# Summing three adaLN modulation vectors on VectorE instead of TensorE, inside the attention of a two-layer diffusion backbone

## The chip, the cores and the metric

The kernel runs on one core of a Trainium2 chip. The metric is the device time of one execution in microseconds (us); lower is better. A core has TensorE (PE, matrix products), VectorE (DVE), ScalarE (ACT), GpSimd (POOL), SyncE (SP) and 16 DMA engines. Each engine works through its own queue in order, and semaphores make the engines wait for each other.

## The reference

A latent stream of 512 tokens and a context of 256 tokens, 1024 wide, all float32, go through two layers. Layer 0 mixes the tokens by multi-head latent attention with 8 heads, layer 1 by a gMLP with spatial gating; each is followed by a squared-ReLU MLP. Every sub-layer is modulated:

```python
m_lat = (silu_c @ ada_w[i] + ada_b[i])
sh_m, sc_m, g_m, sh_f, sc_f, g_f = jnp.split(m_lat, N_MOD, axis=-1)
h_lat = modulate(x, norm_mix_g[i], sh_m, sc_m)
...
x = x + g_m * o_lat
x = x + g_f * squared_relu_mlp(modulate(x, norm_ffn_g[i], sh_f, sc_f), ffn_w1[i], ffn_w2[i])
```

For each layer there are six modulation vectors of 1024 values (shift, scale and gate, for the mixer and for the MLP). Each is the product of one vector, SiLU(c), with a 1024 x 1024 slice of `ada_w`, 4 MB of weights that are used once.

## The kernel before, in words

Activations lie transposed: channels on the 128 partitions, tokens along the free axis, in eight tiles (KT = 8). Products keep float32 accuracy by splitting both operands into a high and a low part and multiplying three times (`mm3`, lines 79 to 82; `split`, lines 70 to 77: ScalarE casts, VectorE subtracts).

The order of the work is the program's order, rearranged by the framework's scheduler, which lets each engine take the instruction of the lowest priority number that is ready by its own timeline. `with later(BG)` (line 197) raises that number by 400, so that the work in it fills holes. `tc.issue_after(ins)` puts an instruction behind `ins` on its engine.

The first two vectors (shift and scale of layer 0's mixer) are formed at the very start. The other ten are background work, written as a generator, `ada_steps` (lines 154 to 188), in the order of line 155. For each vector:

- eight loads of 128 x 1024 weights (512 KB each), issued by GpSimd (line 161) into a ring of `ada_r` buffers, two during the attention (`AR`, line 37) and three later;
- eight accumulations on VectorE (lines 163 and 165) into one buffer, `acc` (`bufs=1`): each weight tile times the value of SiLU(c) that belongs to its row, so that the vector is the sum of `acc` over the partitions;
- that sum, in one of two ways. The first three vectors (n < BGN = 3: the mixer's gate and the MLP's shift and scale of layer 0) are summed on TensorE: eight matmuls with a block of `acc` as the stationary operand and a column of ones as the moving one (line 182), tied behind the last product of probabilities and values issued so far (`bg_state["pe"]`, set in line 692), and one addition of the bias (line 183). The other seven (`fast`) are transposed in blocks of 32 x 32 into an `ada_r` buffer (line 173), summed along the rows into 32 columns (line 174), brought into place by one matmul with a fixed selection matrix (line 175) and completed by four additions of 32 partitions each (line 178).

The generator yields after each load and accumulation; in the first three vectors there is one more step for the sum, in the other seven the sum is in the step of the last load. So a vector is nine steps or eight, and `left` (line 191) counts 80 + 3.

Each step is called by hand. Ahead of the attention's loop `ada_step(8)` (line 722) asks for the first vector's loads; in the loop over 8 heads x 2 halves of the queries (lines 733 to 741), `ada_step(ADS[i])` (line 737) takes 0, 1 or 2 steps, with `ADS` in line 36, 19 in all. With these 27 steps the three vectors of the attention are done: the first is summed at i = 1, the second at i = 7, the third at i = 13. After it, `tick` (line 204) goes on with the other seven during layer 0's MLP.

In the attention's loop `scores` forms the scores of the next half head on TensorE (line 664) and the softmax on VectorE and ScalarE (lines 668 to 673); `values` transposes the probabilities on TensorE (line 686), splits them and multiplies them with the values. Between them are put pieces of the key and value projection (`kv_proj`), of the query projection (`q_proj`) and of the output projection (`out_proj`, whose `residual`, line 631, is the first user of the first of the three vectors). The powers of -0.5 that the norms need are formed on GpSimd (lines 126, 272, 323), on the same queue as the loads of line 161. A key norm's row goes to DRAM and comes back spread over all partitions (lines 277 and 278).

Of the kernel before, what the change touches and what calls it, by code (L numbers as in the profile page):

```python
# [9 lines left out]
F32 = mybir.dt.float32  # L10
# [3 lines left out]
ALU = mybir.AluOpType  # L14
AX = mybir.AxisListType

P = 128
D = 1024
KT = D // P
# [15 lines left out]
BGN = 3  # L35
ADS = [0, 1, 2, 2, 2, 2, 0, 1, 2, 2, 2, 2, 0, 1, 0, 0]
AR = 2, 3
# [9 lines left out]
def hybrid_dit_kernel(  # L47
# [7 lines left out]
    PE, ACT, DVE, POOL = nc.tensor, nc.scalar, nc.vector, nc.gpsimd  # L55
    SBUF, PSUM = bass.MemoryType.SB, bass.MemoryType.PSUM

    def pool(stack, name, bufs=1, space=SBUF, side="left"):
        return stack.enter_context(tc.tile_pool(name=name, bufs=bufs, space=space, side=side, reuse_waits="tile"))

    @contextmanager
    def later(offset):
        with tc.high_priority(offset=-offset):
            yield

    per = pool(ctx, "per")
# [52 lines left out]
    ones = per.tile([P, P], F32, name="ones")  # L119
# [18 lines left out]
    adab = per.tile([P, 96], F32, name="adab")  # L138
    mod = per.tile([P, 2, 6, KT], F32, name="mod")
# [12 lines left out]
    bg_state = {}  # L152

    def ada_steps():
        order = [(0, 2), (0, 3), (0, 4), (0, 5), (1, 0), (1, 1), (1, 2), (1, 3), (1, 4), (1, 5)]
        for n, (l, ch) in enumerate(order):
            fast = n >= BGN
            acc = bg_state["sb"].tile([P, D], F32, tag="ada_acc", bufs=1, name=f"acc{l}{ch}")
            for k in range(KT):
                r = bg_state["sb"].tile([P, D], F32, tag="ada_r", bufs=AR[fast], name=f"adr{l}{ch}{k}")  # L160
                nc.gpsimd.dma_start(out=r, in_=ada_w[l][k * P:(k + 1) * P, ch * D:(ch + 1) * D])  # L161
                if k == 0:
                    DVE.tensor_scalar(out=acc, in0=r, scalar1=sil[:, 0, 0:1], scalar2=None, op0=ALU.mult)
                else:
                    DVE.scalar_tensor_tensor(out=acc, in0=r, scalar=sil[:, k, 0:1], in1=acc, op0=ALU.mult, op1=ALU.add)  # L165
                if k < KT - 1 or not fast:
                    yield
            i = (l * 6 + ch) * KT
            o = bg_state["pt"](f"adr_o{l}{ch}")
            if fast:  # L170
                r = bg_state["sb"].tile([P, D], F32, tag="ada_r", bufs=AR[fast], name=f"adr{l}{ch}t")
                red = per.tile([P, 32], F32, tag="red", bufs=2, name=f"red{l}{ch}")
                DVE.transpose(out=r, in_=acc)
                DVE.tensor_reduce(out=red, in_=r.rearrange("p (b j) -> p b j", j=32), axis=AX.X, op=ALU.add)
                PE.matmul(o[:, :32], lhsT=sel32, rhs=red, start=True, stop=True)
                for q in range(4):
                    s = slice(32 * q, 32 * q + 32)
                    DVE.tensor_tensor(out=mod[s, l, ch, :], in0=o[s, q:32:4], in1=adab[s, i:i + KT], op=ALU.add)
            else:
                with tc.issue_after(bg_state["pe"]):  # L180
                    for b in range(KT):
                        PE.matmul(o[:, b:b + 1], lhsT=acc[:, b * P:(b + 1) * P], rhs=ones[:, :1], start=True, stop=True)
                DVE.tensor_tensor(out=mod[:, l, ch, :], in0=o[:, :KT], in1=adab[:, i:i + KT], op=ALU.add)
            if ch in (1, 4):
                g = (G_MIX if ch == 1 else G_FFN) + l * KT
                DVE.scalar_tensor_tensor(out=mod[:, l, ch, :], in0=mod[:, l, ch, :], scalar=1.0, in1=cols[:, g:g + KT],
                                         op0=ALU.add, op1=ALU.mult)
            yield

    ada = ada_steps()  # L190
    bg_state.update(left=80 + BGN, keep=80 - 8 * BGN)

    def ada_step(n=1):
        for _ in range(n):
            if bg_state["left"] > bg_state["keep"]:
                bg_state["left"] -= 1
                with later(BG):
                    if "after" in bg_state:
                        with tc.issue_after(bg_state["after"]):
                            next(ada)  # L200
                    else:
                        next(ada)
# [124 lines left out]
    def drain(g, n=100):  # L327
        for _ in range(n):
            if next(g, "end") == "end":
                break  # L330

    nka = KVL + ROPE
    with ExitStack() as ini_stack:
# [7 lines left out]
        def pt(name):  # L341
            return ps.tile([P, 512], F32, tag="t", bufs=2, name=name)

        def pa(name):
            return ps.tile([P, 512], F32, tag="a", bufs=6, name=name)
# [56 lines left out]
        with ExitStack() as xstack:  # L402
# [12 lines left out]
            for k in range(0, KT, 2):  # L415
                o = pa(f"xct{k}")
# [4 lines left out]
            for k in range(KT):  # L421
                o = pa(f"xt{k}")
# [18 lines left out]
        for t in range(NT):  # L441
            o = rp[0][:, t * P:(t + 1) * P] if t < 2 else rp[1][:, (t - 2) * P:(t - 1) * P]
# [5 lines left out]
        def make_h(k):  # L448
            xa = inb.tile([P, TOK], F32, tag="xa", bufs=2, name=f"xa{k}")
            ch = inb.tile([P, CTX], F32R, name="ch", bufs=2)  # L450
            cl = inb.tile([P, CTX], F32R, name="cl", bufs=2)
            for j, src, sl, o_h, o_l in ((1, xcT[:, k, :], slice(0, CTX), ch, cl),
                                         (0, xT[:, k, :], slice(CTX, TOK), hh[k], hl[k])):
                A, B = am[:, k, j:j + 1], bm[:, k, j:j + 1]
                DVE.scalar_tensor_tensor(out=xa[:, sl], in0=src, scalar=A, in1=rsb[:, sl], op0=ALU.mult, op1=ALU.mult)
                ACT.activation(out=o_h, in_=xa[:, sl], func=AF.Identity, bias=B)
                DVE.scalar_tensor_tensor(out=o_l, in0=xa[:, sl], scalar=B, in1=o_h.bitcast(F32),
                                         op0=ALU.add, op1=ALU.subtract)
            return ch, cl

        kva = None
        for k in range(KT):
# [6 lines left out]
            ch, cl = make_h(k)  # L469
            for t in range(NT):  # L470
                a_h, a_l = (ch, cl) if t < 2 else (hh[k], hl[k])
                s = bass.ts(t if t < 2 else t - 2, P)
# [5 lines left out]
        for k in range(0, KT, 2):  # L478
            r = W.load(wq_a, k, 2, 0, QL, f"wqa{k}")
# [27 lines left out]
        for u in range(3):  # L507
            st = ini.tile([P, 4, 2], F32, name="kst", bufs=3)
            us = slice(2 * u, 2 * u + 2)
            for j in range(2):  # L510
                t = 2 * u + j
# [4 lines left out]
            o = pt(f"ckt{u}").rearrange("p (k n) -> p k n", k=2)  # L516
            for j in range(2):
                t = 2 * u + j
# [4 lines left out]
            s = slice(2 * u * P, (2 * u + 2) * P)  # L523
# [26 lines left out]
        for t in range(NL):  # L550
            o = qas[t] if t in qas else query_latent(t)
# [83 lines left out]
    with hst as st_:  # L635
# [83 lines left out]
                    residual(0, 2, 2 * dq + d, o, s_)  # L719
                    n0.add(2 * dq + d, half)  # L720

        drain(q_proj(0)); ada_step(8)
        steps = [(h, half) for h in range(HEADS) for half in range(2)]
        scores(0, 0)
        fill = {}
# [133 lines left out]
    with ExitStack() as st_:  # L859
# [7 lines left out]
        for q in range(4):  # L867
            ws = [W(gm_w_in, 2 * k2, 2, HALF + q * 512, 512, f"gv{q}{k2}") for k2 in range(4)]
            for ts in ((0, 1), (2, 3)) if q == 0 else ((0, 1, 2, 3),):
                acc = {t: (pu if t < 2 else pd)(f"v{q}{t}") for t in ts}  # L870
                for k in range(KT):
                    wh, wl = ws[k // 2]
                    for t in ts:
                        s = slice(t * P, (t + 1) * P)
                        mm3(acc[t], hs[k][0][:, s], hs[k][1][:, s], wh[:, k % 2, :], wl[:, k % 2, :], k == 0, k == KT - 1)
                for t in ts:
# [8 lines left out]
                            in_=gm_bs.rearrange("g p -> (g p)").unsqueeze(0).to_broadcast([P, G * P]))  # L885
        for g4 in range(2):
            o = pt(f"wst{g4}")
# [6 lines left out]
            o = pt(f"rsw{g4}")  # L894
# [121 lines left out]
```

## Time and profile before

| | us |
|---|---|
| median of 3 runs | 1373.73 |
| lowest, highest | 1372.16, 1377.34 |
| the profiled execution | 1371.87 |
| its span, first to last instruction | 1370.1 |
| PE busy in the span | 1330.4 (97%) |
| PEld (weight loads) busy | 1138.0 (83%) |
| DVE busy | 850.4 (62%) |
| ACT busy | 536.5 (39%) |
| POOL busy | 88.6 (6%) |

The busy times are of that one execution. PE is TensorE's matmuls and PEld its weight loads, which overlap with matmuls. Matmuls are pipelined and their ends are modelled, so a PE that is busy all the time is not a PE at its peak. The chain of waits follows the work that ended last back from the end: at each step to what released it, or to the instruction before it on its engine. "issue" is time for which the profile shows no cause. "<-" after an idle time names the engine and the tile that ended it.

### The profile page before, as it was taken

The numbers are of one execution on the slowest core, as the hardware profiler recorded it, in microseconds if no ns is written. First come the engines' busy times: TensorE is split into PE (matmuls) and PEld (weight loads), VectorE is DVE, ScalarE is ACT, GpSimd is POOL, SyncE is SP. The second block draws the span as 40 slices with busy tenths as digits, with TensorE's granted clock in tenths as the row PEclk, the third lists the DMA queues.
The fourth block names the chain that finished last, engine by engine and source line by source line (L and its number), as shares of the span: only waits on it lengthen the run. The fifth ranks groups of instructions, "written<-read, shape, count | busy, mean of one in ns | idle before, by whom it ended". The sixth has DMA issues, their size and how long they took to land.

```text
span 1370.1 us, 18200 instructions
## 1 busy us (share of the span) xinstructions
PE 1330.4 (97%) x7055; PEld 1138.0 (83%) x7055; DVE 850.4 (62%) x1409; ACT 536.5 (39%) x1022; POOL 88.6 (6%) x137
## 2 busy tenths in 40 slices
PE   6988899999899999999999999999999999999998
PEld 4888899999888888888897888888888888888888
DVE  5886988888998887434574456445574344343452
ACT  7565566555631322313343333222353132231331
POOL 2031200200111110000000010000000000000000
PEclk9999999999999999999999999999999999999999
DMA  8741411412688876232232232232223233333211
GB/s 267 229 149 61 135 61 53 141 64 74 191 279 267 278 248 214 93 93 92 92 109 92 77 123 77 77 93 92 62 77 111 92 99 98 103 96 94 92 46 62
DMA packets 128070, 166.38 MB, mean 121 GB/s; under 512 B 7643, under 2 KB 111712, under 8 KB 127984
## 3 DMA queue, kind: packets, MB, share of 16 engines
q1 hardware_dynamic: 116032, 122.67, 28.2%
q0 software_dynamic: 11808, 42.03, 9.7%
q8 instruction: 55, 0.90, 0.3%
q10 hardware_dynamic: 144, 0.52, 0.1%
q14 instruction: 31, 0.25, 0.1%
HBM read 163.08 MB, written 2.12 MB: 121 GB/s over the span
## 4 chain that ended last, share of the span: by engine, by line
PE 85%; DVE 4%; issue 4%; DMA 3%; ACT 3%; POOL 0%; SPq 0%; DVEq 0%; ACTq 0%; POOLq 0%
PE s L664 3%; PE v L82 2%; PE v L80 2%; PE v L81 2%; DMA adr<-in_ada_w_dram 1%; PE f1d2o L80 1%; PE f1d0o L81 1%; PE f1d0o L80 1%; PE f1d0o L82 1%; PE f1d2o L81 1%; PE f1d2o L82 1%; PE f0d0o L80 1%; PE f0d1o L81 1%; PE f0d1o L80 1%; PE f0d1o L82 1%
## 5 line engine op out<-in xcount | busy, mean ns | idle before, releaser
L165 DVE SCALAR_TENSOR_TENSOR acc<-adr,sil,acc 128x1024 f32<-128x1024 f32 x70 | 89.6, 1280 | 20.2 <-DMA adr<-in_ada_w_dram 19.8
L161 POOL DMA_DIRECT2D adr<-in_ada_w_dram x80 | 43.0, 538 | 269.3 <-DVE acc L165 121.3
L812 DVE TENSOR_TENSOR f1a<-f1a 128x512 f32<-128x512 f32 (+1 forms) x36 | 22.5, 629 | 39.8 <-ACT f1a L811 39.8
L72 ACT CAST f0uh<-f0a 128x512 fp32r<-128x512 f32 (+1 forms) x36 | 20.4, 572 | 51.4 <-DVE f0a L812 51.4
L668 DVE CUSTOM_DVE_ANT_0 p<-s,rk,rq 128x768 f32<-128x768 f32 x32 | 32.4, 1013 | 8.0 <-DMA rk<-rkd 4.2
L73 DVE TENSOR_TENSOR tl<-pt,th 128x512 fp32r<-128x512 f32 x48 | 31.9, 684 | 6.1 <-ACT th L72 5.8
L671 ACT ACTIVATE p<-p,sm 128x768 f32<-128x768 f32 x32 | 30.1, 941 | 13.3 <-DVE sm L670 13.3
L126 POOL TENSOR_TENSOR nst<-nst,mhalf 128x2 f32<-128x2 f32 x6 | 5.1, 855 | 454.4 <-DVE nst L125 454.4
L73 DVE TENSOR_TENSOR f1ul<-f1a,f1uh 128x512 fp32r<-128x512 f32 (+1 forms) x36 | 22.6, 632 | 18.9 <-ACT f1uh L72 18.6
L812 DVE TENSOR_TENSOR f0a<-f0a 128x512 f32<-128x512 f32 (+1 forms) x36 | 22.5, 627 | 18.2 <-ACT f0a L811 18.2
L72 ACT CAST th<-pt 128x512 fp32r<-128x512 f32 x48 | 26.9, 587 | 17.0 <-PE o L82 9.3
L72 ACT CAST f1uh<-f1a 128x512 fp32r<-128x512 f32 (+1 forms) x36 | 20.5, 572 | 32.0 <-DVE f1a L812 32.0
L73 DVE TENSOR_TENSOR f0ul<-f0a,f0uh 128x512 fp32r<-128x512 f32 (+1 forms) x36 | 22.4, 626 | 11.7 <-ACT f0uh L72 11.7
L81 PE MATMUL o<-tl,vh 128*128 128x256 f32 x96 | 28.2, 294 | 0.0
L80 PE MATMUL o<-th,vh 128*128 128x256 f32 x96 | 28.0, 291 | 0.1
L82 PE MATMUL o<-th,vl 128*128 128x256 f32 x96 | 27.1, 282 | 0.0
L686 PE MATMUL pt<-ident,p 128*128 128x128 f32 x192 | 26.7, 273 | 0.1
L631 DVE SCALAR_TENSOR_TENSOR xT<-wo,mod,xT 128x512 f32<-128x512 f32 (+1 forms) x40 | 25.1, 637 | 2.4 <-PE wo L82 2.1
L922 DVE TENSOR_TENSOR gm<-gm,u 128x512 f32<-128x512 f32 x16 | 11.0, 688 | 20.6 <-ACT u L903 20.5
L686 PEld LDWEIGHTS pt<-ident,p 128*128 128x128 f32 x192 | 22.1, 141 | 1.7 <-DVE p L673 0.8
L664 PE MATMUL s<-kh,qh 128*128 128x384 f32 x64 | 17.5, 355 | 4.8 <-DVE sm L668 4.4
L673 DVE TENSOR_SCALAR p<-p,sm 128x768 f32<-128x768 f32 x32 | 19.8, 617 | 0.6
(2638 smaller groups left out, 4607.2 us busy)
## 6 DMA issues: line engine op xcount, KB each, us to landing
adr<-in_ada_w_dram POOLq DMA_DIRECT2D x80, 512.0 KB, 4.8
rk<-rkd SPq DMA_DIRECT2D x8, 384.0 KB, 3.4
xn<-in_x_dram SPq DMA_DIRECT2D x4, 512.0 KB, 6.9
out_dram<-of SPq DMA_DIRECT2D x8, 256.0 KB, 2.1
xn<-in_ctx_dram SPq DMA_DIRECT2D x2, 512.0 KB, 3.8
ada000r<-in_ada_w_dram SPq DMA_DIRECT2D x1, 512.0 KB
ada001r<-in_ada_w_dram SPq DMA_DIRECT2D x1, 512.0 KB
ada100r<-in_ada_w_dram SPq DMA_DIRECT2D x1, 512.0 KB, 11.4
```

What stands on the lines that cost most here:

```text
L72: ACT.copy(out=hi, in_=src)
L73: eng.tensor_tensor(out=lo, in0=src, in1=hi.bitcast(F32), op=ALU.subtract)
L80: PE.matmul(o, lhsT=wh, rhs=mh, start=start, stop=False)
L81: PE.matmul(o, lhsT=wh, rhs=ml, start=False, stop=False)
L82: return PE.matmul(o, lhsT=wl, rhs=mh, start=False, stop=stop)
L161: nc.gpsimd.dma_start(out=r, in_=ada_w[l][k * P:(k + 1) * P, ch * D:(ch + 1) * D])
L165: DVE.scalar_tensor_tensor(out=acc, in0=r, scalar=sil[:, k, 0:1], in1=acc, op0=ALU.mult, op1=ALU.add)
L664: PE.matmul(S[:, n, :384], lhsT=a, rhs=b[:, n * 384:(n + 1) * 384], start=m == 0, stop=m == 4)
L668: DVE.tensor_tensor_reduce(out=e, in0=S[:, :, :384], in1=rk, op0=ALU.mult, op1=ALU.max, scale=rq, scalar=-3.0e38, accum_out=sm[:, 0:1])
L671: ACT.activation(out=e, in_=e, func=AF.Exp, bias=sm[:, 1:2], accum_out=sm[:, 2:3])
L686: PE.transpose(T[:, j, q * P:(q + 1) * P], Pr[h, 2 * half + q][:, (2 * jp + j) * P:(2 * jp + j + 1) * P], ident)
L812: DVE.tensor_tensor(out=f, in0=f, in1=f, op=ALU.mult)
```

## The change

All ten vectors are summed in the second way. The matmul of the three vectors that are formed during the attention stays tied behind `bg_state["pe"]`. Their vectors become eight steps long, as the others are: the sum is in the step of the last load. So `left` begins at 80, and seven steps instead of eight are taken ahead of the loop. `ADS` stays; its last steps find nothing left to do in the attention. With it the first vector is summed at i = 1, the second at i = 5, the third at i = 11.

```diff
--- before.py
+++ after.py
@@ -163,24 +163,19 @@
                     DVE.tensor_scalar(out=acc, in0=r, scalar1=sil[:, 0, 0:1], scalar2=None, op0=ALU.mult)
                 else:
                     DVE.scalar_tensor_tensor(out=acc, in0=r, scalar=sil[:, k, 0:1], in1=acc, op0=ALU.mult, op1=ALU.add)
-                if k < KT - 1 or not fast:
+                if k < KT - 1:
                     yield
             i = (l * 6 + ch) * KT
             o = bg_state["pt"](f"adr_o{l}{ch}")
-            if fast:
-                r = bg_state["sb"].tile([P, D], F32, tag="ada_r", bufs=AR[fast], name=f"adr{l}{ch}t")
-                red = per.tile([P, 32], F32, tag="red", bufs=2, name=f"red{l}{ch}")
-                DVE.transpose(out=r, in_=acc)
-                DVE.tensor_reduce(out=red, in_=r.rearrange("p (b j) -> p b j", j=32), axis=AX.X, op=ALU.add)
+            r = bg_state["sb"].tile([P, D], F32, tag="ada_r", bufs=AR[fast], name=f"adr{l}{ch}t")
+            red = per.tile([P, 32], F32, tag="red", bufs=2, name=f"red{l}{ch}")
+            DVE.transpose(out=r, in_=acc)
+            DVE.tensor_reduce(out=red, in_=r.rearrange("p (b j) -> p b j", j=32), axis=AX.X, op=ALU.add)
+            with nullcontext() if fast else tc.issue_after(bg_state["pe"]):
                 PE.matmul(o[:, :32], lhsT=sel32, rhs=red, start=True, stop=True)
-                for q in range(4):
-                    s = slice(32 * q, 32 * q + 32)
-                    DVE.tensor_tensor(out=mod[s, l, ch, :], in0=o[s, q:32:4], in1=adab[s, i:i + KT], op=ALU.add)
-            else:
-                with tc.issue_after(bg_state["pe"]):
-                    for b in range(KT):
-                        PE.matmul(o[:, b:b + 1], lhsT=acc[:, b * P:(b + 1) * P], rhs=ones[:, :1], start=True, stop=True)
-                DVE.tensor_tensor(out=mod[:, l, ch, :], in0=o[:, :KT], in1=adab[:, i:i + KT], op=ALU.add)
+            for q in range(4):
+                s = slice(32 * q, 32 * q + 32)
+                DVE.tensor_tensor(out=mod[s, l, ch, :], in0=o[s, q:32:4], in1=adab[s, i:i + KT], op=ALU.add)
             if ch in (1, 4):
                 g = (G_MIX if ch == 1 else G_FFN) + l * KT
                 DVE.scalar_tensor_tensor(out=mod[:, l, ch, :], in0=mod[:, l, ch, :], scalar=1.0, in1=cols[:, g:g + KT],
@@ -188,7 +183,7 @@
             yield
 
     ada = ada_steps()
-    bg_state.update(left=80 + BGN, keep=80 - 8 * BGN)
+    bg_state.update(left=80, keep=80 - 8 * BGN)
 
     def ada_step(n=1):
         for _ in range(n):
@@ -719,7 +714,7 @@
                     residual(0, 2, 2 * dq + d, o, s_)
                     n0.add(2 * dq + d, half)
 
-        drain(q_proj(0)); ada_step(8)
+        drain(q_proj(0)); ada_step(7)
         steps = [(h, half) for h in range(HEADS) for half in range(2)]
         scores(0, 0)
         fill = {}
```

## Rows read from the trace of the kernel before

**Rows 1.** The page's 40 slices: tenths busy.

```profile
PE   6988899999899999999999999999999999999998
...
DVE  5886988888998887434574456445574344343452
```

**Rows 2.** Attention by stretch: us; PE, PEld, DVE, ACT, POOL busy (x); PEclk; DMA; GB/s.

```profile
100.00:120.00 20.00, 15.29 (x91) 14.17 (x90) 12.19 (x38) 12.50 (x52) 4.22 (x4) 0.83 0.26 86
120.00:140.00 20.00, 19.48 (x130) 18.36 (x129) 14.55 (x35) 12.39 (x30) 0.00 (x0) 1.00 0.08 25
140.00:180.00 40.00, 35.93 (x249) 33.84 (x249) 37.63 (x89) 25.48 (x79) 9.12 (x11) 1.00 0.45 137
180.00:240.00 60.00, 60.00 (x408) 57.15 (x407) 48.08 (x120) 36.57 (x109) 5.47 (x5) 1.00 0.15 50
240.00:260.00 20.00, 18.69 (x127) 16.93 (x126) 16.61 (x28) 10.02 (x31) 5.05 (x7) 1.00 0.63 193
260.00:320.00 60.00, 60.00 (x386) 56.20 (x386) 51.18 (x125) 34.41 (x94) 4.69 (x4) 1.00 0.19 62
```

**Rows 3.** The chain that ended last, 230 to 262 us: start, length, what.

```profile
236.67 1.46 PE adr_o L182 x14
...
253.25 0.54 DVE acc L165
...
255.68 1.27 DVE acc L165
```

**Rows 4.** The same chain over the whole span, its longest pieces.

```profile
119.56 27.65 issue
...
324.28 1.45 PE adr_o L182 x14
```

**Rows 5.** Instructions of line 182: min/median/max ns, first and last start.

```profile
L182 PEld LDWEIGHTS adr_o<-ones,acc x48: 188/192/193, 143.5 to 325.5; 128*128 128x128 f32 x48
L182 PE MATMUL adr_o<-ones,acc x48: 164/250/250, 143.6 to 325.5; 128*128 128x1 f32 x48
```

**Rows 6.** Instructions of lines 173 to 178, in the vectors formed later.

```profile
L173 DVE STREAM_TRANSPOSE adr05t<-acc x1: 1234/1234/1234, 391.0 to 391.0; 128x1024 f32<-128x1024 f32 x1
...
L174 DVE TENSOR_REDUCE red<-adr05t x1: 1204/1204/1204, 392.8 to 392.8; 128x32 f32<-128x1024 f32 x1
...
L175 PEld LDWEIGHTS adr_o<-red,sel x14: 187/188/189, 408.4 to 575.6; 128*128 128x128 f32 x14
L175 PE MATMUL adr_o<-red,sel x14: 190/232/275, 408.6 to 575.6; 128*128 128x32 f32 x14
...
L178 DVE TENSOR_TENSOR mod<-adr_o,adab x28: 143/162/172, 410.1 to 576.8; 32x8 f32<-32x8 f32 x28
```

**Rows 7.** VectorE in order of time, the first, a middle and the last stretch.

```profile
94.07 1.27 DVE L165 SCALAR_TENSOR_TENSOR acc<-adr,sil,acc 128x1024 f32<-128x1024 f32 x1
...
110.79 0.42 DVE L304 COPY qn<-q 128x256 f32<-128x256 f32 x1 [5.04 <-ACT junk L303]
...
146.18 0.74 DVE L163 TENSOR_SCALAR acc<-adr,sil 128x1024 f32<-128x1024 f32 x1
...
170.19 1.28 DVE L165 SCALAR_TENSOR_TENSOR acc<-adr,sil,acc 128x1024 f32<-128x1024 f32 x1
...
239.95 1.28 DVE L165 SCALAR_TENSOR_TENSOR acc<-adr,sil,acc 128x1024 f32<-128x1024 f32 x1
```

**Rows 8.** GpSimd in order of time, 60 to 352 us.

```profile
95.64 0.53 POOL L161 DMA_DIRECT2D adr<-in_ada_w_dram  x1 [1.83 <-DVE acc L165]
...
99.29 1.33 POOL L272 TENSOR_TENSOR st<-st,mhalf 128x6 f32<-128x6 f32 x1 [2.51 <-DVE st L271]
...
118.39 1.17 POOL L323 TENSOR_TENSOR rq<-rq,mhalf 128x4 f32<-128x4 f32 x1 [3.82 <-DVE rq L322]
...
239.54 0.59 POOL L161 DMA_DIRECT2D adr<-in_ada_w_dram  x1 [19.02 <-DVE sm L672]
240.19 2.25 POOL L272 TENSOR_TENSOR st<-st,mhalf 128x6 f32<-128x6 f32 x1
```

## The prediction

> **What bounds the kernel now.** I read the page's slices first, then the attention cut into stretches, then the chain of waits. In the slices TensorE stands at nine tenths or more almost everywhere; VectorE stands near that from the first slices to about the sixteenth, so in the attention (some 100 to 340 us) two engines are nearly full at once [rows 1]. The stretches say where each of them is the one that waits. From 180 to 240 and from 260 to 320 us TensorE is busy throughout and VectorE has 11.9 and 8.8 us left over. From 140 to 180 us it is the other way round: VectorE is busy 37.6 of 40 us and TensorE lacks 4.1. From 240 to 260 TensorE lacks 1.3 with VectorE at 16.6 of 20. From 100 to 120 us neither is full: TensorE lacks 4.7 and runs at a mean granted clock of 0.83 (a mix of its levels of 1.2 and 2.4 GHz), and VectorE is free for 7.8; in the next 20 us it is free for 5.5 [rows 2].
>
> The chain runs through the work that is changed in two ways: the matmuls of line 182 stand on it near 236 and 324 us, and accumulations of line 165 stand on it at 253 and 255 us [rows 3, 4]. Near 120 to 147 us the chain shows only "issue", so it doesn't say whether the first vector's matmuls at 143.5 us count there.
>
> **Removed from TensorE.** Eight matmuls of a vector are 16 weight loads and 16 matmuls in the trace, 48 of each for three vectors [rows 5]. Their durations overlap, so I price them by what the chain gives: 14 of them take 1.46 us [rows 3], 0.104 each, so 16 take 1.67 us. In their place come two records for a vector (14 for the seven vectors that are summed so already), at 0.232 us each if nothing overlaps [rows 6]: 0.46. That is 1.2 us less per vector at the least and, at the old spacing of 0.104, 1.46 at the most. Two of the three blocks are shown on the chain, so I take two at 1.35 (between the two ends), **-2.7 us**; all three at 1.46 would be -4.4, and one at 1.2 the low end.
>
> A rule of the Trainium skill would price this higher. Its page "Perfetto Trace Analysis", section "Identifying the Most-Contended Engine", asks to judge TensorE by the busy share of its weight loads. By that, 48 loads of 0.192 less 6 of 0.188 free 8.1 us, and the sum below would end some 5 us lower. The chain contradicts it: 14 loads and matmuls pass in 1.46 us though 14 loads alone add up to 2.7.
>
> **Added to VectorE.** For each vector a transpose of 1.234, a row sum of 1.204 and three more small additions than now (four of 0.162 take the place of one) [rows 6]: 2.92 us, 8.8 for three. Nothing is wholly free here; the ends are 0 (all in VectorE's idle time) and +8.8 (all on the path).
>
> **Moved.** This is the part that decides where those 8.8 us lie. Now a vector's accumulator stays taken until its matmuls, which are tied behind a step's last value matmul. The first vector's last accumulation ran near 94 us, the second vector's first at 146 [rows 7], right after the first block of matmuls, while the load at 95.64 us, the tenth, was already its second [rows 8]. With the change the transpose frees the accumulator, and only the last small matmul stays tied. So the second vector can follow the first at once, in the stretch with 13.3 us of idle VectorE (100 to 140), and the third can follow the second, where the second lies now (146 to 171), instead of starting at 239.54. Step by step:
> - First vector's finish, 2.9 us of VectorE near 96 to 111 us: VectorE sits idle there for 5.04 us in one piece, waiting on ScalarE [rows 7]. I cost it at nothing; without that gap it is +2.9.
> - Second vector: 9.7 us of accumulations (0.74 and seven of about 1.28) go, as far as loads allow, from the full stretch into the idle one. I count no gain, because the third vector's accumulations then want the place that they leave.
> - The second finish (2.9 us) then falls in or near 140 to 180 us, where VectorE is full and TensorE waits for it. I cost it in full, **+2.9 us**.
> - Third vector: its accumulations leave 239 to 257 us. Two of them stand on the chain there, 0.54 and 1.27 us [rows 3], so **-1.8 us**; the most that the stretch can give is about that and the lost 1.3 us of TensorE.
> - The third finish falls in 180 to 240 or 260 to 320 us, with 11.9 and 8.8 us of VectorE to spare: nothing; +2.9 if it lands in a full piece.
> - The transposed copy takes one of the two load buffers between a vector's last load and the next vector's second; the load that waits for it waits one transpose and one row sum, 2.4 us, off the path as long as nobody needs the vector soon. The first vector is first used by the output projection of the first head pair, several steps later.
> - The 24 loads stay 24 loads of the same size. Nothing after the attention changes: the other seven vectors are summed as before.
>
> The sum: -2.7 + 2.9 - 1.8 = -1.6 us. The profiled execution took 1371.87 us (span 1370.1), 1.9 below the median of 1373.73; against the median the sum gives **1372.1 us**.
>
> **Rivals.** *Faster: VectorE's relief is real.* If the second vector leaves the full stretch and the third doesn't fill it, TensorE gets back the 4.1 us that it lacks there; with all three matmul blocks (-4.4) and the 1.8 us, it is -10.3 and 1363.4. For it: the idle 13.3 us lie just ahead, and 9.7 us of accumulations fit. Against it: the order on VectorE is made by a scheduler that puts this background work into any hole it sees, so the third vector should move up too. It decides as soon as TensorE's idle time from 140 to 180 us falls below about 1 us.
>
> *Slower: GpSimd's queue at the head of the attention.* The loads of these vectors are issued by GpSimd, in order, and each waits until VectorE has freed a buffer (1.83 us ahead of the one at 95.64). On the same queue between 99 and 119 us stand four powers, the square roots of the first keys and queries (the first at 99.29, the last at 118.39) [rows 8], and no load stands among them now, because the accumulator is taken. If the second vector moves up, its loads stand in front of them: four waits of 1.83 and four issues of 0.53 are +9.4 us before the first softmax, and the time is 1372.1 + 9.4 = 1381.5. For it: TensorE already starves from 100 to 120 us, so nothing covers it. Against it: loads and powers sit in turn on that queue now as well. It decides above 8.5 us of extra wait, where the 1.6 us of gain and the half per cent are used up.
>
> A power that meets an accumulation also lasts longer: 2.25 us at 240.19, with an accumulation begun at 239.95, against 1.33 for the same power at 99.29 [rows 7, 8]. The Trainium skill says why in "SBUF — State Buffer", section "Who interferes with whom": a VectorE instruction with two SBUF inputs keeps GpSimd from reading SBUF. By that rule this rival would cost four times 0.92 us more, 1385 in all, and the added transposes and row sums, with one input each, would cost GpSimd nothing; the lengthened power agrees, the second half no row here shows.
>
> *No effect of the move:* the scheduler leaves the loads where they are, only the finish differs, and VectorE's idle time takes it: -2.7, 1371.0. This lies inside the forecast's half per cent.
>
> **How the numbers follow.** A measurement of this kernel can tell about 0.5% (6.9 us) from no change. The forecast with the rival of no move has 0.60 and spans 1366.9 to 1380.6: all 8.8 us exposed with one block gained is +7.6 - 1.8 = 1379.5, none exposed with three blocks is -6.2. Faster has 0.20, slower 0.20. The range takes in both rivals' own times, 1363 to 1382.
>
> **What would show it.** Right: some 42 fewer weight loads on TensorE; VectorE's sum 8 to 9 us higher; accumulations of the second vector between 96 and 146 us; none of line 165 between 239 and 257; chain without adr_o pieces of 1.46 us. The step on 140 to 180 us is wrong if TensorE's idle time there shrinks; the step on the start is wrong if the last of the four powers, now at 118.39 us, comes more than 2 us later. The whole is wrong if the attention's end moves by more than 7 us either way, or if the stretch behind it, which is not touched, changes by more than that.

## The result, and the profile after

| us | before | after |
|---|---|---|
| median | 1376.2 (5 runs) | 1385.63 (5 runs) |
| lowest, highest | 1372.16, 1378.32 | 1383.95, 1387.11 |
| the profiled execution, its span | 1371.87, 1370.1 | 1383.95, 1382.2 |

The kernel became slower: the ratio is 1.0071 [1.0055, 1.0087]. Below, a ratio is also given in microseconds, as its distance from 1 times the 1376 us of the kernel before: here +9.8 [7.6, 12.0]. The forecast was 1372.1, in a range of 1363 to 1382; it stood on the 1373.73 us of three runs, and against its own base it said -1.6.

Where the time went is read in this order. The page's sums of the kernel after, busy us and instructions of each engine:

```profile
PE 1331.6 (96%) x7013; PEld 1135.7 (82%) x7013; DVE 858.7 (62%) x1424; ACT 538.2 (39%) x1022; POOL 87.7 (6%) x137
```

and of the kernel before:

```profile
PE 1330.4 (97%) x7055; PEld 1138.0 (83%) x7055; DVE 850.4 (62%) x1409; ACT 536.5 (39%) x1022; POOL 88.6 (6%) x137
```

There are 42 weight loads fewer and as many matmuls fewer; VectorE has 8.3 us more. The edit did what it says. The powers of line 126 date the loss: the first ends the attention, the last stands in layer 1. The row of that line, before:

```profile
L126 POOL TENSOR_TENSOR nst<-nst,mhalf x6: 695/700/1624, 342.9 to 1010.2; 128x2 f32<-128x2 f32 x6
```

and after:

```profile
L126 POOL TENSOR_TENSOR nst<-nst,mhalf x6: 696/700/1623, 354.2 to 1022.3; 128x2 f32<-128x2 f32 x6
```

The attention ends 11.3 us later, the last power comes 12.1 later, and the span is 12.1 us longer: in these two executions nearly all of the loss is made before the attention's end.

Next, the attention in stretches, after, beside [rows 2]:

```profile
100.00:120.00 20.00, 12.64 (x58) 10.57 (x57) 15.12 (x33) 9.25 (x38) 8.57 (x10) 0.74 0.70 222
120.00:140.00 20.00, 14.17 (x88) 12.14 (x87) 17.49 (x37) 10.29 (x31) 4.29 (x6) 1.00 0.56 182
140.00:180.00 40.00, 34.52 (x214) 32.67 (x215) 36.08 (x87) 22.36 (x65) 5.14 (x6) 0.91 0.26 79
180.00:240.00 60.00, 59.62 (x401) 56.43 (x400) 47.51 (x121) 36.27 (x108) 4.66 (x4) 1.00 0.16 49
240.00:260.00 20.00, 20.00 (x143) 19.30 (x142) 14.41 (x33) 13.61 (x40) 1.32 (x1) 1.00 0.14 45
```

TensorE is idle for 7.36 and 5.83 us in the first two stretches (4.71 and 0.52 before). The 1.3 us at 240 to 260 have come back, as forecast. And the DMA share, 0.70 and 0.56 against 0.26 and 0.08, tells that far more weights are loaded there than before. Over all of 100 to 320 us TensorE's idle time grows from 10.6 to 19.0 us, by 8.4. Before:

```profile
100.00:320.00 220.00, 209.39 (x1381) 196.65 (x1380) 180.25 (x430) 131.37 (x393) 28.56 (x30) 0.98 0.26 83
```

and after:

```profile
100.00:320.00 220.00, 200.96 (x1290) 187.43 (x1289) 178.98 (x430) 127.95 (x382) 28.79 (x31) 0.96 0.27 83
```

Then, when each vector was finished, after (line 172 is the transpose):

```profile
L172 DVE STREAM_TRANSPOSE adr02t<-acc x1: 1234/1234/1234, 96.4 to 96.4; 128x1024 f32<-128x1024 f32 x1
L172 DVE STREAM_TRANSPOSE adr03t<-acc x1: 1233/1233/1233, 126.4 to 126.4; 128x1024 f32<-128x1024 f32 x1
L172 DVE STREAM_TRANSPOSE adr04t<-acc x1: 1233/1233/1233, 153.7 to 153.7; 128x1024 f32<-128x1024 f32 x1
```

The second vector did follow the first at once, 101 to 125 us. So did the third, 130 to 153: the scheduler did all three in a row, while the forecast had the third where the second lay before (146 to 171).

VectorE in order of time, after; the last figure in brackets is idle time and what ended it:

```profile
110.78 1.28 DVE L165 SCALAR_TENSOR_TENSOR acc<-adr,sil,acc 128x1024 f32<-128x1024 f32 x1 [1.85 <-DMA adr<-in_ada_w_dram]
114.05 1.28 DVE L165 SCALAR_TENSOR_TENSOR acc<-adr,sil,acc 128x1024 f32<-128x1024 f32 x1 [1.99 <-DMA adr<-in_ada_w_dram]
115.25 0.42 DVE L299 COPY qn<-q 128x256 f32<-128x256 f32 x1
...
126.41 1.23 DVE L172 STREAM_TRANSPOSE adr03t<-acc 128x1024 f32<-128x1024 f32 x1
...
131.47 1.00 DVE L663 CUSTOM_DVE_ANT_0 p<-s,rk,rq 128x768 f32<-128x768 f32 x1
```

The first copy of a query (line 299, 304 before), which came at 110.79 in [rows 7], comes at 115.25, 4.5 us later. Of these, 1.2 us are the accumulation at 114.05 and its wait, which stand ahead of it: ScalarE's squares of that query, which ended VectorE's wait in the kernel before, were done at 114.03. The other 3.3 us were lost before, on TensorE's queue. There the queries' product stands behind the transposition of a key norm, which waits for GpSimd's power. Before:

```profile
105.15 1.33 POOL L272 TENSOR_TENSOR st<-st,mhalf 128x6 f32<-128x6 f32 x1 [4.53 <-DVE st L271]
106.53 0.08 PEld L274 LDWEIGHTS rkt<-ident,st 128*6 128x6 f32 x1 [2.54 <-POOL st L272]
```

and after:

```profile
107.18 0.15 DVE L266 SCALAR_TENSOR_TENSOR st<-st,epk 128x6 f32<-128x6 f32 x1
107.25 1.28 DVE L165 SCALAR_TENSOR_TENSOR acc<-adr,sil,acc 128x1024 f32<-128x1024 f32 x1
107.43 2.32 POOL L267 TENSOR_TENSOR st<-st,mhalf 128x6 f32<-128x6 f32 x1 [0.66 <-DVE st L266]
109.80 0.08 PEld L269 LDWEIGHTS rkt<-ident,st 128*6 128x6 f32 x1 [3.90 <-POOL st L267]
```

VectorE feeds this power 2.3 us later than before, and the power, beside an accumulation, takes 2.32 us instead of 1.33. The first product of the softmax (line 663, 668 before) comes at 131.47. In the kernel before, in the same view:

```profile
121.21 1.02 DVE L668 CUSTOM_DVE_ANT_0 p<-s,rk,rq 128x768 f32<-128x768 f32 x1
```

That is 10.3 us later. It is near what the whole kernel loses, but the experiments show that the two don't go together one to one. The chain of waits of the kernel after, 100 to 140 us, shows in shares what stands ahead of it:

```profile
by line: DMA adr<-in_ada_w_dram 55.3%; DVE acc L165 16.2%; issue 14.4%; DVE red L173 2.8%; POOL rq L318 2.6%; DVE rl L541 2.1%; DVE cq_l L76 2.0%; DVE vl L73 1.6%; POOL adr L161 1.5%; DVE kl L76 1.2%; DVE wqb01l L73 1.2%; DVE wqb02l L73 1.2
...
106.18 4.50 DMA adr<-in_ada_w_dram
...
110.78 1.30 DVE acc L165
...
112.36 4.28 DMA adr<-in_ada_w_dram
...
116.73 1.30 DVE acc L165
```

Background work is most of the chain there, where before, from 119.56 us on, it held a single piece without a cause [rows 4]. Each of the two loads shown, of 4.50 and 4.28 us, starts when an accumulation has freed one of the two buffers, and a later accumulation waits for it. One may be tempted to read the 55% of DMA as the cause; the runs below without the loads and with the second vector alone say how far that holds.

### The profile page after: what moved, and what is told of

The parts are those of the page before. It is cut to its first block, busy times and chain, and to the rows that moved or that the text cites. A ratio compares the mean times of both kernels' runs of the same rounds, so it can differ in the third digit from the quotient of the medians.

```text
span 1382.2 us, 18129 instructions
## 1 busy us (share of the span) xinstructions
PE 1331.6 (96%) x7013; PEld 1135.7 (82%) x7013; DVE 858.7 (62%) x1424; ACT 538.2 (39%) x1022; POOL 87.7 (6%) x137
## 4 chain that ended last, share of the span: by engine, by line
PE 81%; DMA 7%; DVE 7%; issue 3%; ACT 3%; POOL 0%; SPq 0%; DVEq 0%; ACTq 0%; POOLq 0%
DMA adr<-in_ada_w_dram 6%; PE s L659 3%; PE v L80 2%; PE v L82 2%; PE v L81 2%; DVE acc L165 1%; PE pt L681 1%; PE f1d2o L81 1%; PE f1d0o L82 1%; PE f1d0o L80 1%; PE f1d2o L80 1%; PE f1d0o L81 1%; PE f1d2o L82 1%; PE f0d2o L81 1%; PE f1d1o L82 1%
```

## The experiments

### Hold the two vectors back, and keep the new sum

Against the kernel after: each of the second and third vectors starts behind the last bias addition of the one ahead of it. Nothing else changes.

```diff
-                    DVE.tensor_scalar(out=acc, in0=r, scalar1=sil[:, 0, 0:1], ...)
+                    with tc.issue_after(last) if n in TIED else nullcontext():
+                        DVE.tensor_scalar(out=acc, in0=r, scalar1=sil[:, 0, 0:1], ...)
...
-                DVE.tensor_tensor(out=mod[s, l, ch, :], in0=o[s, q:32:4], ...)
+                last = DVE.tensor_tensor(out=mod[s, l, ch, :], in0=o[s, q:32:4], ...).ins
```

> The changed kernel, with the first accumulation of the second and of the third vector put behind the bias addition of the vector before it, so that the accumulations can't run ahead; the sums on VectorE stay as changed. Theory 'move' (the early accumulations at the head of the attention cost the time): 1371 to 1377 us, at or below the kernel before, and TensorE's idle time from 100 to 160 us back from 16 to about 7 us. Theory 'sum' (the added 8.7 us of transposes and row sums cost it wherever they stand): 1383 to 1388 us, as the changed kernel.

1.0024 [1.0014, 1.0035], +3.3 us: two thirds of the loss are gone, and the time lies between the two expectations. TensorE's idle time from 100 to 160 us is back from 16.4 to 7.2 us, as the theory of the move had it. The first softmax product is at 122.96 us, 8.5 earlier than in the kernel after. What is left shows in the stretches of this kernel:

```profile
180.00:240.00 60.00, 55.38 (x358) 50.37 (x357) 53.12 (x120) 33.22 (x100) 9.53 (x10) 1.00 0.32 99
```

TensorE lacks 4.6 us here, none before: the third vector, eight steps long now, lies at 206 to 236 instead of 239 to 265 (the prediction's 257 leaves out its last two accumulations, at 259 and 264).

### The same sum in the kernel before

The kernel before, with the transpose, row sum, one matmul and four additions for all ten vectors; nine steps as before, and the next vector held behind the bias addition as above, so that accumulations stay where they were.

```diff
-            if fast:
+            if True:
...
-                PE.matmul(o[:, :32], lhsT=sel32, rhs=red, start=True, stop=True)
+                with nullcontext() if fast else tc.issue_after(bg_state["pe"]):
+                    PE.matmul(o[:, :32], lhsT=sel32, rhs=red, start=True, stop=True)
```

> The kernel before with nothing changed but the sum: transposes and row sums on VectorE and one matmul, in the steps of before (finish at i = 1, 7 and 13), and the next vector's accumulations held until the bias addition, as the matmuls of before held them. Doubling the sums cost some 4 us for 7.3 us of VectorE, which gives 4.4 us for the 8.7 us here. If the 42 matmul records that go are worth the 2.7 us that the prediction gave them: 1.7 us over the kernel before, -0.5 to +3. If they were hidden anyway: 4.4 over it, +3 to +6.

1.0003 [0.9992, 1.0014], +0.4 us. The new sum alone costs nothing that can be measured. The second vector starts at its old place, and so does the third:

```profile
146.92 0.75 DVE L165 TENSOR_SCALAR acc<-adr,sil 128x1024 f32<-128x1024 f32 x1
...
241.04 0.75 DVE L165 TENSOR_SCALAR acc<-adr,sil 128x1024 f32<-128x1024 f32 x1
```

With both back there, the whole loss of 9.8 us is gone. The kernel after has the same sum and differs from this one only in where the work lies: it has no hold, and eight steps for a vector instead of nine. That is 9.4 us. The experiment ahead has the hold and eight steps, so these 9.4 fall into 6.5 us for running ahead of the hold and 2.9 for the shorter steps, which put the third vector some 35 us earlier even where it is held. (A difference of two of these ratios is good to 2 or 3 us.)

### One matmul of eight: TensorE's term by itself

The kernel before, with one matmul of 8 columns for a vector in place of eight.

```diff
-                    for b in range(KT):
-                        PE.matmul(o[:, b:b + 1], lhsT=acc[:, b * P:(b + 1) * P], rhs=ones[:, :1], ...)
+                    PE.matmul(o[:, :KT], lhsT=acc[:, :P], rhs=ones[:, :KT], ...)
```

> The kernel before with one of the eight matmuls of each of the three vectors left in (8 columns wide); it leaves out the sum over the other seven blocks. This measures the TensorE term alone. If the prediction's price holds (1.2 to 1.46 us for each block, two or three blocks on the path): 2.4 to 4.4 us under the kernel before. If other work hides them: within 1 us of it.

0.9981 [0.9971, 0.9991], -2.6 us, for 42 loads and 42 matmuls fewer, as many as the change removes. VectorE's price is then the difference to the experiment ahead: 0.4 + 2.6 = 3.0 us, give or take 2.

### Leave the new sum's VectorE work out, keep the move

Against the kernel after, for the three vectors:

```diff
-            DVE.transpose(out=r, in_=acc)
-            DVE.tensor_reduce(out=red, in_=r.rearrange("p (b j) -> p b j", j=32), ...)
+            DVE.tensor_copy(out=red, in_=acc[:, :32])
```

> The changed kernel; it leaves out the block transposes and row sums of the three vectors of the attention (a copy of 32 columns stands in their place), so VectorE has some 7 us less to do while the accumulations still run ahead. Theory 'move': still slow, 1380 to 1386 us. Theory 'sum': 1372 to 1377 us.

1.0044 [1.0029, 1.0060], +6.1 us, within what the theory of the move asked, and the first softmax product at 134.3: most of the loss stays without the transposes and row sums. That part is neither their work nor a wait for them. The 3.7 us that went are near VectorE's price of 3.0.

### Leave the loads of the two vectors out: GpSimd's queue

Against the kernel after, the accumulations of the second and third vector read the resident identity matrix; their 16 loads, and with them the loads' issues on GpSimd's queue, are gone.

```diff
-                r = bg_state["sb"].tile([P, D], F32, tag="ada_r", ...)
-                nc.gpsimd.dma_start(out=r, in_=ada_w[l][k * P:(k + 1) * P, ...])
+                if n in (1, 2):
+                    r = ident.unsqueeze(1).to_broadcast([P, KT, P])
+                else:
+                    ...
```

> The changed kernel; it leaves out the sixteen weight loads of the second and third vector, whose accumulations of the same size read a tile that is resident instead, and may run ahead as in the changed kernel. If what costs the time is that VectorE and GpSimd, in order, stand still for weights that have not landed or buffers that are not free ('waiting'): 1372 to 1377 us. If it is that VectorE is occupied by 20 us of accumulations at a place where the attention needs it ('occupation'): 1381 to 1387 us.

1.0033 [1.0019, 1.0048], +4.5 us, just below what was expected of 'occupation', with the first softmax product at 133.8 us, later still than in the kernel after. This run bears on GpSimd's queue. That queue in this kernel, 95 to 135 us (line 273 is the power of a key, 324 that of a query):

```profile
102.44 1.34 POOL L273 TENSOR_TENSOR st<-st,mhalf 128x6 f32<-128x6 f32 x1 [5.18 <-DVE st L272]
109.93 1.33 POOL L273 TENSOR_TENSOR st<-st,mhalf 128x6 f32<-128x6 f32 x1 [6.16 <-DVE st L272]
119.73 1.91 POOL L324 TENSOR_TENSOR rq<-rq,mhalf 128x4 f32<-128x4 f32 x1 [8.46 <-DVE rq L323]
126.54 2.85 POOL L324 TENSOR_TENSOR rq<-rq,mhalf 128x4 f32<-128x4 f32 x1 [4.89 <-DVE rq L323]
```

and in the kernel after:

```profile
102.52 1.36 POOL L267 TENSOR_TENSOR st<-st,mhalf 128x6 f32<-128x6 f32 x1
...
107.43 2.32 POOL L267 TENSOR_TENSOR st<-st,mhalf 128x6 f32<-128x6 f32 x1 [0.66 <-DVE st L266]
...
118.86 1.05 POOL L318 TENSOR_TENSOR rq<-rq,mhalf 128x4 f32<-128x4 f32 x1
...
126.59 1.03 POOL L318 TENSOR_TENSOR rq<-rq,mhalf 128x4 f32<-128x4 f32 x1 [1.09 <-DVE rq L317]
```

with VectorE's steps that feed the last two powers there:

```profile
118.47 0.16 DVE L317 TENSOR_SCALAR rq<-rq 128x4 f32<-128x4 f32 x1
...
126.34 0.16 DVE L317 TENSOR_SCALAR rq<-rq 128x4 f32<-128x4 f32 x1
```

Without a single load in between, the last power starts at 126.54 instead of 126.59, and GpSimd has been idle for 4.89 us, waiting for VectorE. In the kernel after, too, each of the four powers starts within 0.4 us of the end of the step on VectorE that feeds it (here 0.23 and 0.09 us). The powers are late because VectorE's inputs for them are late; their order behind loads is not what holds them. VectorE, in order, has 19.86 of 20 us of work at 100 to 120 in this kernel (12.19 before). What goes with the loads is the second share, 9.8 - 4.5 = about 5 us. It is felt behind the first softmax: TensorE's idle time from 120 to 180 us is 7.9 us here and 11.3 in the kernel after. The nearest cause is VectorE's waiting for them; that it is the whole share isn't shown, since the run takes away the loads' traffic and their issues as well. The waits of VectorE, 94 to 180 us, after:

```profile
DVE acc L165 <- DMA adr<-in_ada_w_dram: 8.0, 8, 2.0
```

that is 8.0 us in 8 waits, in which all that stands behind an accumulation waits too. In the kernel before it was:

```profile
DVE acc L165 <- DMA adr<-in_ada_w_dram: 0.5, 1, 0.5
```

### Hold only the third vector

As the first experiment, with `TIED = (2,)` in place of `(1, 2)`.

> The changed kernel with the third vector alone held behind the second one's bias addition; the second still runs ahead at the head of the attention. If the second vector's early accumulations are the cost: within 2 us of the changed kernel, 7 to 11 us over the kernel before. If the third's are: as e1_tied, 2 to 5 us over it.

1.0047 [1.0034, 1.0060], +6.5 us, just below what was expected if the second vector is the whole cost. Read as a ladder: the sum alone +0.4, both held with eight steps +3.3, only the third held +6.5, neither +9.8. Taken in this order, the shorter steps, the second vector's running ahead and the third's cost some 3 us each.

The ladder also shows what the late first softmax is worth. It comes here at

```profile
131.66 1.00 DVE L665 CUSTOM_DVE_ANT_0 p<-s,rk,rq 128x768 f32<-128x768 f32 x1
```

as late as in the kernel after, and with both held at

```profile
122.96 1.02 DVE L665 CUSTOM_DVE_ANT_0 p<-s,rk,rq 128x768 f32<-128x768 f32 x1
```

These 8.7 us become 3.2 at the end. TensorE's idle time follows the end better than the first softmax does (softmax and idle time of one profiled execution each, against the kernel before; that of the sum alone was 3.1 us above its median):

| | first softmax product, us later | TensorE idle, 100 to 320 us, more | time, us more |
|---|---|---|---|
| the kernel after | 10.3 | 8.4 | 9.8 |
| the sum alone | 1.7 | 2.6 | 0.4 |
| both held | 1.8 | 3.0 | 3.3 |
| only the third held | 10.5 | 7.3 | 6.5 |
| without the new sum's VectorE work | 13.1 | 6.4 | 6.1 |
| without the loads | 12.6 | 6.1 | 4.5 |

### The sum done twice

The first experiment's kernel, with the transpose and row sum of the three vectors doubled.

```diff
-            DVE.transpose(out=r, in_=acc)
-            DVE.tensor_reduce(out=red, ...)
+            for _ in range(1 if fast else 2):
+                DVE.transpose(out=r, in_=acc)
+            for _ in range(1 if fast else 2):
+                DVE.tensor_reduce(out=red, ...)
```

> As e1_tied, with the transpose and the row sum of each of the three vectors done twice (7.3 us more on VectorE). Theory 'move': 0 to 3 us over e1_tied. Theory 'sum': 6 to 8 us over it.

1.0051 [1.0038, 1.0065], 3.7 us over the kernel that it doubles, for 3 x (1.23 + 1.21) = 7.3 us of VectorE. It falls between the two expectations: half of it is covered. Half of the 8.8 us that the prediction counted would be 4.4; 3.0 was found.

### The move without the new sum

The prediction's expected layout, second vector early and third at the old place of the second, with the sums still on TensorE: the kernel before with a second accumulator. The room for it is made by a raw weight ring of 3 buffers in place of 4, which alone is the control.

```diff
-PM, PS, PT, OB, BG, RB = 2, 1, 3, 4, 400, 4
+PM, PS, PT, OB, BG, RB = 2, 1, 3, 4, 400, 3
```

> The kernel before with three instead of four buffers for raw weights, which frees 4 KB of each partition. The control for e10_ring3_early: 1375 to 1379 us, the kernel before or up to 3 us over it.

The control missed its expectation: 1.0057 [1.0042, 1.0072], +7.8 us, with the first softmax product 7.2 us late. Its loss lies ahead of the attention: TensorE is busy for 42.9 of the first 60 us, against 47.8 before. Which wait causes it wasn't tested; ScalarE's waits for the raw `ada_w` tiles grow from 7.2 to 13.9 us there. With the second accumulator on top:

```diff
-            acc = bg_state["sb"].tile([P, D], F32, tag="ada_acc", bufs=1, ...)
+            acc = bg_state["sb"].tile([P, D], F32, tag="ada_acc", bufs=1 if fast else 2, ...)
```

> As e9_ring3, with two accumulators instead of one; the sums stay on TensorE. The second vector's accumulations run ahead to the head of the attention and the third's lie where the second's lay: the layout that the prediction expected of the change, without any of its sums. If the move is the cost, whatever forms the sums: 3 to 9 us over e9_ring3, the first softmax product at 129 to 134 us instead of 121. If the prediction's pricing of the move was right: 0 to 4 us under e9_ring3.

1.0112 [1.0097, 1.0127], +15.4; against its control the quotient is 1.0055, or +7.6 us. The end came as expected of the move, the first softmax product (139.98 us) later than the 129 to 134 expected. The second vector lay at 104 to 128 us, the third at 164 to 190, and sums stayed on TensorE. Row sums, transposes, their buffers and the third vector's haste are all absent, and the loss is there. The first softmax product in the control:

```profile
128.40 1.02 DVE L668 CUSTOM_DVE_ANT_0 p<-s,rk,rq 128x768 f32<-128x768 f32 x1
```

and with the second vector early:

```profile
139.98 1.02 DVE L668 CUSTOM_DVE_ANT_0 p<-s,rk,rq 128x768 f32<-128x768 f32 x1 [0.58 <-PE s L664]
```

It is 11.6 us later, against 10.3 in the change itself, and VectorE's waits for loads from 94 to 180 us grow from 1.7 us in the control to 8.5. This is the same mechanism, without the new sum and with the steps of before; on a slower base, so its size carries over only roughly.

### Two other places for the transposes

The kernel with the sum alone, with the transposes of all three vectors also held behind the step's last split on VectorE (the first then runs at 145.06 us instead of 98.04):

```diff
+                with nullcontext() if fast else tc.issue_after(bg_state["dve"]):
+                    DVE.transpose(out=r, in_=acc)
...
-            split(O, Os[h][0][:, s], Os[h][1][:, s])
+            bg_state["dve"] = split(O, Os[h][0][:, s], Os[h][1][:, s]).ins
```

> As e5_sum_only, with the transpose also held behind the last split of the step's values on VectorE, so that no transpose or row sum stands at the head of the attention (97 to 101 us). If the first vector's sum costs the 1.8 us there by which the first softmax product came late in e1_tied (123.0 against 121.2 us): 1 to 3 us under e5_sum_only. If VectorE's idle piece near 105 us takes it, as the prediction had it: within 1 us of e5_sum_only.

1.0054 [1.0041, 1.0067], +7.4 us: both expectations missed. The waits of TensorE in this kernel, 100 to 345 us, name one new cost:

```profile
PE adr_o L179 <- DVE red L177: 3.1, 2, 2.4
```

The small matmul, tied in order on TensorE, now waits 2.4 us at the longest for the row sum behind that split. That accounts for 3.1 of the 7.4 at the most; the rest stays open. The expectation's premise was wrong, too. In the run with one matmul of eight, which has no transpose and no row sum there, the first softmax product is as late as with both vectors held, and the first vector's first accumulation, ahead of any sum, is already 1.8 us later than in the kernel before (73.01):

```profile
74.77 0.74 DVE L163 TENSOR_SCALAR acc<-adr,sil 128x1024 f32<-128x1024 f32 x1
...
122.80 1.02 DVE L667 CUSTOM_DVE_ANT_0 p<-s,rk,rq 128x768 f32<-128x768 f32 x1
```

From the one to the other it is 48.0 us in that run, 48.1 with the sum alone and 48.2 in the kernel before. So the first vector's transpose and row sum don't delay the first softmax where they stand in the sum alone, as the prediction had it.

The kernel with the sum alone, with the first transpose held behind the key statistics of the second head, that is in VectorE's idle piece of [rows 7]:

```diff
+                with tc.issue_after(bg_state["dve"]) if n == 0 else nullcontext():
+                    DVE.transpose(out=r, in_=acc)
...
+        if h == 1:
+            bg_state["dve"] = ins
```

> As e5_sum_only, with the first vector's transpose held behind the statistics of head 1's keys, so that the transpose and the row sum fall into VectorE's idle piece near 105 to 111 us. If that piece takes them, as the prediction had it: first softmax product at 121 to 122 us instead of 123 and 1 to 2 us under e5_sum_only, 1 to 2 under the kernel before. If not: as e5_sum_only.

1.0014 [1.0002, 1.0026], +1.9 us. The transpose ran at 105.54 and the first softmax product came at 121.73, in the expected range, but the end did not follow. The 1.2 us by which it comes earlier than with the sum alone aren't the transpose's: the first accumulation begins at 73.30 here and at 74.86 there, and from it to the softmax it is 48.4 us against 48.1. No version with the whole sum came out below the kernel before; the run with one matmul of eight, at -2.6 us, bounds what the idea could give if VectorE's part cost nothing.

## Why the prediction was wrong

**The step that failed is "Moved".** It let 9.7 us of accumulations go "from the full stretch into the idle one" and counted that at 0, and it counted the third vector's departure from 239 to 257 at -1.8. Measured, the move is +9.4 us (the change against the sum alone) and some +7.6 in the layout that the prediction had in mind. For the steps, eight instead of nine, the prediction had no term; 2.9 of the 9.4 us go with them. The 13.3 us of idle VectorE at 100 to 140 us were real, but not spare. They lay between the short steps of the first keys and queries, on which the first softmax waits; TensorE, idle for 4.7 us there [rows 2], was waiting too. An engine that runs in order can't let a 0.42 us copy pass a 1.28 us accumulation, much less one that still waits up to 2.0 us for its load. So the idle time was filled, and the work between it slid: first softmax product +10.3 us, and TensorE idle for 13.2 us from 100 to 140, 8.0 more than before.

Such a delay reaches the end only as far as TensorE's later idle time can't give it back. Before, that was 4.1 us from 140 to 180 and 1.3 from 240 to 260. With only the third vector held, 140 to 180 gives back 2.7 us and 240 to 260 all of its 1.3 (180 to 240, where the third vector then lies, loses 4.8); in the kernel after, accumulations of the third vector still stand in 140 to 153, and 140 to 180 loses 1.4 more. That the whole loss is so near the 10.3 us of the first softmax is, by the other runs, chance.

**Right:** TensorE's -2.7 (measured -2.6, between -4.0 and -1.2). The chain was the better price. The Trainium skill's "Perfetto Trace Analysis", section "Identifying the Most-Contended Engine", names the weight loads' busy share, beside the share of peak work, as a measure of TensorE's headroom; taken as the price of the loads that go, as the prediction tried, it would have been 8.1. VectorE's +2.9 is right in size (3.0, give or take 2). Which of the three finishes it comes from isn't shown: doubling costs half of the added work, while the prediction had one finish of three exposed in full. The two terms' sum, nearly nothing, is what the sum alone gives (+0.4). Of the -1.8, TensorE's idle time at 240 to 260 shows 1.3 (to none), and it drowned. Nothing behind the attention changed by more than 0.8 us.

**The slower rival** had the place, the head of the attention, and nearly the size: +9.4 for the first softmax, which came 10.3 us later; 7.8 over its base for the end, against 9.8. But its mechanism was GpSimd's queue, and the powers are as late without loads, and in the kernel after within 0.4 us of their inputs. Its other part, powers lengthened by accumulations, did happen: to one of the four, by 1.0 us, not to all, and that one stands on TensorE's way to the first queries (107.43 to 109.80). Its sign that the last power would come over 2 us later (126.59 against 118.39) was fulfilled by another cause: a delay seen on a queue doesn't say that the queue makes it.

The faster rival needed TensorE's idle time at 140 to 180 us to fall below 1 us; it grew from 4.1 to 5.5, as the late softmax moved into it. The rival of no move is refuted by the times of the transposes.

**Open:** how the loss divides between the second and third vector if held in another order; what the smaller weight ring delays; how much of the loads' share is VectorE's waiting; why the two other places of the transposes cost what they do. Each edit also lets the scheduler reorder other work, so single differences of 1 or 2 us are not read as costs of one instruction.

## What to carry to other kernels

Look for what an edit stops holding back: here a buffer that came free earlier let the scheduler run two vectors of background work some 45 and 110 us ahead, and one step less for each vector moved them too; together that cost 9.4 us, while the exchange of operations, on which most of the thought went, was worth 0.4. Idle time of an in-order engine in front of a chain of short dependent steps is not room for long background work; before counting it as cover, ask what follows each piece, and whether the engine that sets the end has idle time left to return a delay. When an edit frees a buffer that held other work back, put another hold in its place: a tie of the next vector's start brought back 6.5 of 9.8 us. And a late first step is not yet a loss of the same size: 8.7 us at the first softmax became 3.2 at the end.

## What the runs showed of the hardware

Granted clock: it was lower in two of the stretches in which TensorE was idle for longer than before, 0.74 on average at 100 to 120 us (0.83 before) and 0.91 at 140 to 180 (1.00 before), but not in the third, 120 to 140, where 5.83 us of idle time against 0.52 left it at 1.00. In pieces of 5 us, after:

```profile
105.00:110.00 5.00, 1.03 (x5) 0.49 (x5) 3.92 (x7) 1.02 (x4) 3.16 (x3) 0.50 0.77 254
110.00:115.00 5.00, 5.00 (x17) 5.00 (x17) 2.23 (x2) 1.10 (x5) 0.84 (x2) 0.50 0.66 196
```

and before:

```profile
105.00:110.00 5.00, 3.47 (x12) 3.47 (x13) 0.55 (x2) 0.60 (x3) 1.33 (x1) 0.50 0.30 101
110.00:115.00 5.00, 5.00 (x31) 4.93 (x30) 2.97 (x12) 3.04 (x14) 1.11 (x1) 0.98 0.19 60
```

0.50 is 1.2 GHz. After, TensorE had been busy for 2.29 us at 100 to 105 and 1.03 at 105 to 110; then it worked for 5 us without a gap at the lower level. Products of the queries follow each other at 0.32 us there (110.30, 110.62) and at 0.18 at the higher one (111.10, 111.28 in the kernel before). From 105 to 115 us the busy time at the lower level is 6.0 us, against some 3.5 before; as an estimate from these rows, that costs some 1 us more, which TensorE's idle time doesn't show.

A power on GpSimd beside an accumulation was again longer: 2.32 us for a key at 107.43 (an accumulation began at 107.25), against 1.36 for the one at 102.52; and 1.91 and 2.85 us for a query in the run without loads (accumulations began at 119.50 and 126.37), against 1.11 and 1.17 in the kernel before. The one at 126.59 in the kernel after, beside a transpose begun at 126.41, took 1.03. The Trainium skill's "SBUF — State Buffer", section "Who interferes with whom", names two SBUF inputs as the condition; this transpose has one, and the second half of the rule, which no row before could show, agrees in this one row.
